# Fewer and wider matmuls per weight block in a hybrid encoder, with the two halves of a sum joined afterwards

## The chip, the core and the metric

The kernel runs on one core of one Trainium2 chip. The metric is the device time of one execution in microseconds, as the median of several runs. The engines have these names in all rows: PE is the matrix engine and PEld its weight load, DVE the vector engine, ACT the scalar engine, POOL the general-purpose one, SP the one that issues most transfers. DMA stands for the 16 transfer engines that all queues share.

## What is computed

Four residual layers over 256 tokens of width 1024, all in float32. Layer i has token mixer i mod 3 (so A, B, C, A), and after it a dense SwiGLU mixer; each has an RMS norm ahead and a residual sum behind.

```python
def short_conv_mixer(h, w_in, conv_w, w_out):              # mixer A
    b_gate, c_gate, u = jnp.split(h @ w_in, 3, axis=-1)
    return (b_gate * depthwise_conv3(c_gate * u, conv_w)) @ w_out

def hyena_mixer(h, w_in, short_w, short_b, ..., w_out):     # mixer C
    v, x1, x2 = jnp.split(depthwise_conv3(h @ w_in, short_w, short_b), 3, axis=-1)
    z = x1 * long_conv(v, 0)
    z = x2 * long_conv(z, 1)
    return z @ w_out

def swiglu(h, w13, w2):
    g, u = jnp.split(h @ w13, 2, axis=-1)
    return (jax.nn.silu(g) * u) @ w2

def reference(x, ...):
    for i in range(DEPTH):                                  # 4
        h = rmsnorm(x, norm_mix_g[i])
        x = x + mixer(i % 3)(h, ...)                        # A, B, C, A
        x = x + swiglu(rmsnorm(x, norm_ffn_g[i]), f_w13[i], f_w2[i])
    return x
```

Mixer B is neighbourhood attention on a 4 x 64 grid. The hidden width of the SwiGLU mixer is 2816. The long convolutions of mixer C use filters that a small network makes from positions.

## The kernel before

Activations lie transposed: 128 features on the partitions, 256 tokens (`T`) along them, eight such tiles for the width of 1024 (`KT`) and 22 for the hidden width (`FT`).

**Split numbers.** Each float32 operand is cut into a rounded part `hi` and a remainder `lo`, both of the type fp32r, and a product is the sum of three: `hi` of the weight with both parts of the input, and `lo` of the weight with the first part. `mm3` (L119) issues these as three matmuls of 256 columns for a block, that is, for one 128x128 piece of a weight. All three add into the same 256 columns of a PSUM bank.

**A weight's way.** `wload` (L96) takes the next of five buffers `st`, and SP issues the transfer of up to 512 KB into it. ACT makes `hi` by a cast (L106). `lo` is made in one of three ways: DVE subtracts (L114 by the helper at L75), POOL does the same, or ACT writes the negative and POOL issues a transfer that reads the weight from memory a second time and adds it (L109, L110). Six buffers each hold `hi` and `lo`, so PE works on one weight while five lie ahead of it. In the SwiGLU mixers of layers 0 and 1, 17% of the weights go to POOL (`POOL_FILTERS`), until the last two output tiles. In mixer C nearly all go the third way (`low_dma`). All others go to DVE.

**Stages.** `ffn` (L265) runs 11 steps `j`, each of four weights (two of the gate, two of the other half) into two banks, `pg` and `pu`, and `gated` follows each: two products with the norm's factor `R` on DVE, Silu on ACT, the product of both on DVE, and the split into `hid`. Then `po` sums 22 blocks for each of the eight output tiles, three weights a tile. `mixer_a` has three weights for each of eight tiles `m` (`ai`), its own `gated`, and then the output projection `OutProj`. `mixer_c` has 24 weights `ci`, each pair followed by `short`, and spectra, gates and inverse transforms between them. In layers 0 and 1 `fill` puts a piece of the filter network (`filters`, tiles `ff`, `fl`, `fh`) behind some steps. In mixer B and in `OutProj` the activations or the sums are laid out otherwise.

**Order.** Eight PSUM banks serve all stages. `Pipeline` puts `gated` and the like behind the weight of a later tick. The instructions stand on each engine in an order that a scheduler makes from the program, and each engine takes its own in that order.

Of the kernel before, what the change touches and what calls it, by code (L numbers as in the profile page):

```python
# [18 lines left out]
P = 128  # L19
D = 1024  # L20
# [26 lines left out]

POOL_FILTERS = 0.17
# [4 lines left out]
def encoder(ctx: ExitStack, tc: tile.TileContext, A: dict, out: bass.AP):  # L53
# [40 lines left out]
    share, count, low_dma = [0], [0], [False]  # L94

    def wload(src, n, tag="", cuts=((0, None, None),)):  # L96
# [5 lines left out]
        for c0, c1, then in cuts:  # L102
# [16 lines left out]
    def mm3(ps, w, ws, xh, xl, first, last, skip=False):  # L119
# [4 lines left out]
        pe.matmul(ps, lo[:, ws], xh, start=False, stop=last, **kw)  # L124

# [139 lines left out]
    def ffn(layer, norm, nxt, fill):  # L265
        with tc.tile_pool(name=f"ffn{layer}", bufs=NP_) as hp:
            hid = []

            def gated(j, pg, pu):
                if j == 0:  # L270
                    norm.expand()
                tg, tu = t2(f"tg{layer}_{j}"), t2(f"tu{layer}_{j}")
                tt(v2(tg), v2(pg), norm.R2(), ALU.mult)
                sg = t2(f"sg{layer}_{j}")
                ac.activation(sg, tg, AF.Silu)
                tt(v2(tu), v2(pu), norm.R2(), ALU.mult)
# [7 lines left out]
            line = Pipeline()
            for j in range(NP_):
                pg, pu = bank(f"pg{layer}_{j}"), bank(f"pu{layer}_{j}")
                parts = []
                for ps, base in ((pg, 0), (pu, FT)):
                    for i in range(2):
                        c = base + 2 * j + i  # L290
                        w = wload(A["f_w13"][layer, c], D, f"w13_{layer}_{c}")
                        parts.append((ps[:, i * T : (i + 1) * T], w, i == 0))
                        if j == 0 and len(parts) == 4:
                            in_group(parts, norm)
                        elif j:
                            in_tile(*parts[-1][:2], norm)
                        line.tick()
                if j == 0:
                    line.add(line.now + NORM_LAG, norm.stats)
                line.add(line.now + (NORM_LAG + 1) * (j == 0), gated, j, pg, pu)  # L300
            while line.todo:
                line.tick()
            for m in range(KT):
# [3 lines left out]
                for k0, k1 in ((0, 8), (8, 15), (15, 22)):  # L307
                    w = wload(A["f_w2"][layer, m][:, k0 * P : k1 * P], (k1 - k0) * P, f"w2_{layer}_{m}_{k0}")
                    for k in range(k0, k1):
                        h = hid[k // 2][:, k % 2]  # L310
                        mm3(ps[:, :T], w, slice((k - k0) * P, (k - k0 + 1) * P), h[:, 0], h[:, 1],
                            k == 0, k == FT - 1)
# [5 lines left out]
    def triple(w, m, norm, name, ready, each=lambda i: None):  # L318


        a, b = bank(f"{name}a{m}"), bank(f"{name}b{m}")
        parts = []
        for i, ps in enumerate((a[:, :T], a[:, T:], b[:, :T])):
            if i == 0 and isinstance(ready, tuple):
                wt = ready
# [611 lines left out]
```

## Time and profile before

| | us |
|---|---|
| median of 3 runs | 1228.61 (1228.05 to 1230.01) |
| the profiled execution | 1226.87 |
| its span in the trace | 1225.1 |
| PE busy in the span | 1206.4 |
| DVE busy | 889.6 |
| ACT busy | 639.5 |
| POOL busy | 186.2 |

The span goes from the first to the last instruction of the trace; 1.8 us of the execution lie outside it. Stages follow each other on PE in this order: mixer A of layer 0 from 6 to 102 us, SwiGLU 0 to 304, mixer B to 425, SwiGLU 1 to 625, mixer C to 750, SwiGLU 2 to 939, mixer A of layer 3 to 1032, SwiGLU 3 to the end. A busy share counts an engine as busy while an instruction runs, so a pipelined engine can be 98% busy and still have room between the starts of its instructions: for PE one reads the distance from start to start.

### The profile page before, as it was taken

To read this page: it belongs to the slowest core of one execution; us is meant where nothing else is said; L and a number is where in the kernel's file an instruction comes from. 1 tells how busy PE (TensorE), PEld (TensorE's weight loads), DVE (VectorE), ACT (ScalarE), POOL (GpSimd) and SP (SyncE) were. 2 spreads that over 40 slices of the span, in tenths; PEclk is the share of its full clock that TensorE was granted. 3 is DMA by queue.
4 is the path that set the end of the run, shared out by engine and by line. 5 is a ranking of instruction groups with operands and counts; after the bars stand their busy time and mean duration, and the time that the engine had idled before them with its cause. 6 is when DMAs were issued, how large, how long until landed. Compare 5 with 4: busy or idle time off the path is not lost.

```text
span 1225.1 us, 24409 instructions
## 1 busy us (share of the span) xinstructions
PE 1206.4 (98%) x10034; PEld 1200.5 (98%) x10034; DVE 889.6 (73%) x1209; ACT 639.5 (52%) x916; POOL 186.2 (15%) x175
## 2 busy tenths in 40 slices
PE   7999999999998999999999999999999999999998
PEld 7999999999998999999999999999999999999998
DVE  7867877988676778788849996766654886766642
ACT  6445554555566655545558675444444444544431
POOL 0001122232454122222322110000000000000000
PEclk9999999999999999999999999999999999999999
DMA  8556656667666456665689995655665655655661
GB/s 316 183 178 206 201 168 207 175 200 223 218 182 188 147 191 187 195 192 175 208 256 288 293 280 192 221 183 178 176 187 173 207 181 161 204 182 186 169 200 44
DMA packets 72104, 242.00 MB, mean 198 GB/s; under 512 B 10231, under 2 KB 11641, under 8 KB 71865
## 3 DMA queue, kind: packets, MB, share of 16 engines
q1 hardware_dynamic: 61408, 211.68, 54.8%
q0 software_dynamic: 8256, 22.84, 8.1%
q10 hardware_dynamic: 2328, 5.93, 1.3%
q8 instruction: 78, 1.28, 0.4%
q14 instruction: 34, 0.27, 0.1%
HBM read 234.10 MB, written 6.29 MB: 196 GB/s over the span
## 4 chain that ended last, share of the span: by engine, by line
PE 91%; DVE 2%; DMA 2%; POOL 2%; ACT 1%; issue 1%; SPq 0%; POOLq 0%; DVEq 0%; ACTq 0%
PE pu L122 7%; PE pg L122 7%; PE pg L124 7%; PE pu L123 7%; PE pg L123 7%; PE pu L124 7%; PE po L124 7%; PE po L123 7%; PE po L122 7%; PE ci L123 2%; PE ci L122 2%; PE ci L124 2%; PE ai1a L123 1%; PE ai1a L122 1%; PE ai1a L124 1%; PE ai0a L123 1%
## 5 line engine op out<-in xcount | busy, mean ns | idle before, releaser
L106 ACT CAST hiw<-stw 128x1024 fp32r<-128x1024 f32 (+1 forms) x276 | 280.5, 1024 | 315.7 <-PE pg L123 82.4
L75 DVE TENSOR_TENSOR low<-stw,hiw 128x1024 fp32r<-128x1024 f32 (+1 forms) x254 | 305.2, 1208 | 156.8 <-ACT hiw L106 155.4
L122 PE MATMUL pu<-xsf,hiw 128*128 128x256 f32 x704 | 199.9, 284 | 0.0
L122 PE MATMUL pg<-xsf,hiw 128*128 128x256 f32 x704 | 199.3, 283 | 0.0
L124 PE MATMUL pg<-xsf,low 128*128 128x256 f32 x704 | 199.2, 283 | 0.0
L123 PE MATMUL pu<-xsf,hiw 128*128 128x256 f32 x704 | 199.2, 283 | 0.0
L123 PE MATMUL pg<-xsf,hiw 128*128 128x256 f32 x704 | 199.2, 283 | 0.0
L124 PE MATMUL pu<-xsf,low 128*128 128x256 f32 x704 | 199.2, 283 | 0.0
L123 PE MATMUL po<-hid,hiw 128*128 128x256 f32 x704 | 197.5, 281 | 0.0
L122 PE MATMUL po<-hid,hiw 128*128 128x256 f32 x704 | 197.5, 281 | 0.0
L124 PE MATMUL po<-hid,low 128*128 128x256 f32 x704 | 197.5, 281 | 0.0
L122 PEld LDWEIGHTS pg<-xsf,hiw 128*128 128x128 f32 x704 | 134.6, 191 | 0.3 <-issue 0.3
L122 PEld LDWEIGHTS pu<-xsf,hiw 128*128 128x128 f32 x704 | 134.5, 191 | 0.3 <-ACT hiw L106 0.3
L124 PEld LDWEIGHTS pg<-xsf,low 128*128 128x128 f32 x704 | 134.6, 191 | 0.0
L123 PEld LDWEIGHTS pg<-xsf,hiw 128*128 128x128 f32 x704 | 134.6, 191 | 0.0
L123 PEld LDWEIGHTS pu<-xsf,hiw 128*128 128x128 f32 x704 | 134.6, 191 | 0.0
L124 PEld LDWEIGHTS pu<-xsf,low 128*128 128x128 f32 x704 | 134.6, 191 | 0.0
L122 PEld LDWEIGHTS po<-hid,hiw 128*128 128x128 f32 x704 | 132.4, 188 | 0.0
L123 PEld LDWEIGHTS po<-hid,hiw 128*128 128x128 f32 x704 | 132.4, 188 | 0.0
L124 PEld LDWEIGHTS po<-hid,low 128*128 128x128 f32 x704 | 132.4, 188 | 0.0
L75 POOL TENSOR_TENSOR low<-stw,hiw 128x1024 fp32r<-128x1024 f32 (+1 forms) x22 | 53.5, 2432 | 215.3 <-ACT hiw L106 207.3
L106 ACT CAST hiai<-stai 128x1024 fp32r<-128x1024 f32 (+1 forms) x49 | 49.0, 1014 | 58.4 <-issue 26.6
(246 smaller groups left out, 2795.4 us busy)
## 6 DMA issues: line engine op xcount, KB each, us to landing
stw<-in_f_w SPq DMA_DIRECT2D x208, 512.0 KB, 3.6
stw<-in_f_w SPq DMA_DIRECT2D x64, 448.0 KB, 3.5
stai<-in_a_w_in SPq DMA_DIRECT2D x45, 512.0 KB, 3.6
stbi<-in_b_w_qkv SPq DMA_DIRECT2D x24, 512.0 KB, 4.3
stci<-in_c_w_in SPq DMA_DIRECT2D x24, 512.0 KB, 8.2
loci<-in_c_w_in POOLq DMA_DIRECT2D x19, 512.0 KB, 16.8
stao<-in_a_w_out SPq DMA_DIRECT2D x16, 512.0 KB, 3.4
hf<-ht POOLq DMA_DIRECT2D x16, 256.0 KB, 2.7
```

The source lines that it names most:

```text
L75: (eng or ve).tensor_tensor(out=out_, in0=a, in1=b, op=op)
L106: ac.copy(out=hi[:, c], in_=st[:, c])
L122: pe.matmul(ps, hi[:, ws], xh, start=first, stop=False, **kw)
L123: pe.matmul(ps, hi[:, ws], xl, start=False, stop=False, **kw)
L124: pe.matmul(ps, lo[:, ws], xh, start=False, stop=last, **kw)
```

## The change

- `mm2` replaces `mm3` in the SwiGLU mixers (both products), in the input products of mixers A and C. A block now has two matmuls: `hi` of the weight with both parts of the input side by side, 512 columns into a whole bank, and `lo` with the first part, 256 columns into the first half. `OutProj`, mixer B and the filter network keep three.
- The second half of the bank has to be added. `join` does it for the input products: ACT copies the half to SBUF, DVE adds the other half to it. For `po` DVE adds both halves to `X` one after the other.
- `ffn` runs 22 steps of two weights, with a bank for the gate and one for the other half. `gated` works on 256 columns where it worked on 512, but for the product with `R`. Mixer A takes three banks for each tile where it took two, mixer C two where it took one.
- No `lo` is made on POOL any more. In the SwiGLU mixers of layers 0 and 1, 34% of the weights (`DMA_FILTERS`) get it from ACT and the adding transfer.

```diff
-POOL_FILTERS = 0.17
+DMA_FILTERS = 0.34
...
-            if low_dma[0]:
+            count[0] += 1
+            if int(count[0] * share[0]) > int((count[0] - 1) * share[0]) and not isinstance(src, list):
                 ac.activation(lo[:, c], st[:, c], AF.Copy, scale=-1.0)
                 gp.dma_start(out=lo[:, c], in_=src[:, c], accum_op=ALU.add)
-                continue
...
+            else:
+                tt(lo[:, c], st[:, c], hi[:, c].bitcast(F32), ALU.subtract)
...
+    def mm2(ps, w, ws, hl, first, last):
+        hi, lo = w
+        pe.matmul(ps, hi[:, ws], hl.rearrange("p s t -> p (s t)"), start=first, stop=False)
+        pe.matmul(ps[:, :T], lo[:, ws], hl[:, 0], start=False, stop=last)
+
+    def join(dst, ps, name):
+        c = t1(name)
+        ac.copy(out=c, in_=ps[:, T:])
+        tt(dst, ps[:, :T], c, ALU.add)
...
-            def gated(j, pg, pu):
+            def gated(j, ps):
...
+                s = t2(f"s{layer}_{j}")
+                for i in range(2):
+                    join(s[:, i * T : (i + 1) * T], ps[i], f"c{layer}_{j}{i}")
+                tt(v2(s), v2(s), norm.R2(), ALU.mult)
+                sg = t1(f"sg{layer}_{j}")
+                ac.activation(sg, s[:, :T], AF.Silu)
+                hh = t1(f"hh{layer}_{j}")
+                tt(hh, sg, s[:, T:], ALU.mult)
...
+                split(pair[-1][:, j % 2], hh)
...
-                        mm3(ps[:, :T], w, slice((k - k0) * P, (k - k0 + 1) * P), h[:, 0], h[:, 1],
-                            k == 0, k == FT - 1)
+                        mm2(ps, w, slice((k - k0) * P, (k - k0 + 1) * P), hid[k], k == 0, k == FT - 1)
+                tt(X[:, m, :], X[:, m, :], ps[:, T:], ALU.add)
                 residual(m, ps[:, :T], nxt)
...
-                tt(v2(bc), v2(a), norm.R2(), ALU.mult)
-                tt(u, b[:, :T], norm.R, ALU.mult)
+                for i, dst in enumerate((bc[:, :T], bc[:, T:], u)):
+                    join(dst, ps[i], f"c{ia}_{m}{i}")
+                tt(v2(bc), v2(bc), norm.R2(), ALU.mult)
+                tt(u, u, norm.R, ALU.mult)
...
-                tt(v2(pr), v2(ps), norm.R2(), ALU.mult)
+                for j in range(2):
+                    join(pr[:, j * T : (j + 1) * T], ps[j], f"c{q}_{i}{j}")
+                tt(v2(pr), v2(pr), norm.R2(), ALU.mult)
```

Three places show how the instructions stand. A row has the line of its own kernel, the operation, what it writes and reads, and the size of what it writes.

On PE, the start of a gate product in SwiGLU 0 (`xsf` is the split input, `hiw13` and `low13` are the parts of a weight). Before:

```order
L122 MATMUL pg0_2_1616<-xsf0_0_1216,hiw13_0_4_1619 128x256
L123 MATMUL pg0_2_1616<-xsf0_0_1216,hiw13_0_4_1619 128x256
L124 MATMUL pg0_2_1616<-xsf0_0_1216,low13_0_4_1620 128x256
L122 MATMUL pg0_2_1616<-xsf0_2_1227,hiw13_0_4_1619 128x256
L123 MATMUL pg0_2_1616<-xsf0_2_1227,hiw13_0_4_1619 128x256
L124 MATMUL pg0_2_1616<-xsf0_2_1227,low13_0_4_1620 128x256
```

Now:

```order
L128 MATMUL pg0_2_1318<-xsf0_0_1104,hiw13_0_2_1321 128x512
L129 MATMUL pg0_2_1318<-xsf0_0_1104,low13_0_2_1322 128x256
L128 MATMUL pg0_2_1318<-xsf0_2_1115,hiw13_0_2_1321 128x512
L129 MATMUL pg0_2_1318<-xsf0_2_1115,low13_0_2_1322 128x256
L128 MATMUL pg0_2_1318<-xsf0_4_1128,hiw13_0_2_1321 128x512
```

Two rows stand where three stood, 2688 times in the program, and the columns of a block are 768 as before.

On DVE, the middle of SwiGLU 2, four weights long (`tg`, `tu` are the two halves times `R`, `hh` the gated product, `hid` the remainder of its split). Before:

```order
L75 TENSOR_TENSOR tg2_6_10499<-pg2_6_10334,Rf2_9759 128x512
L75 TENSOR_TENSOR low13_2_37_10572<-stw13_2_37_10570,hiw13_2_37_10571 128x1024
L75 TENSOR_TENSOR low13_2_16_10604<-stw13_2_16_10602,hiw13_2_16_10603 128x1024
L75 TENSOR_TENSOR tu2_6_10500<-pu2_6_10335,Rf2_9759 128x512
L75 TENSOR_TENSOR hh2_6_10505<-sg2_6_10502,tu2_6_10500 128x512
L75 TENSOR_TENSOR low13_2_17_10645<-stw13_2_17_10643,hiw13_2_17_10644 128x1024
L75 TENSOR_TENSOR hid2_6_10507<-hh2_6_10505,hid2_6_10507 128x2x256
L75 TENSOR_TENSOR low13_2_38_10675<-stw13_2_38_10673,hiw13_2_38_10674 128x1024
```

Now, two weights long (`s` holds the joined halves, `c2` what ACT copied out of a bank):

```order
L74 TENSOR_TENSOR s2_7_9264<-pg2_7_9179,c2_70_9265 128x256
L74 TENSOR_TENSOR s2_7_9264<-pu2_7_9180,c2_71_9268 128x256
L74 TENSOR_TENSOR s2_7_9264<-s2_7_9264,Rf2_8930 128x512
L74 TENSOR_TENSOR low13_2_33_9462<-stw13_2_33_9460,hiw13_2_33_9461 128x1024
L74 TENSOR_TENSOR hh2_7_9274<-sg2_7_9272,s2_7_9264 128x256
L74 TENSOR_TENSOR s2_8_9324<-pg2_8_9240,c2_80_9325 128x256
L74 TENSOR_TENSOR s2_8_9324<-pu2_8_9241,c2_81_9328 128x256
L74 TENSOR_TENSOR hid2_6_9215<-hh2_7_9274,hid2_6_9215 128x256
L74 TENSOR_TENSOR s2_8_9324<-s2_8_9324,Rf2_8930 128x512
L74 TENSOR_TENSOR low13_2_12_9486<-stw13_2_12_9484,hiw13_2_12_9485 128x1024
```

Five small instructions come with two weights where four larger ones came with four, and the sums that free the banks now wait for ACT's copy as well as for PE.

On POOL, a stretch of SwiGLU 0 (`l`, `lr`, `sk`, `eo`, `hf` belong to the filter network). Before:

```order
L75 TENSOR_TENSOR lr00_2385<-l100_2084,lr00_2385 128x256
L75 TENSOR_TENSOR low13_0_14_2345<-stw13_0_14_2343,hiw13_0_14_2344 128x1024
L640 DMA sk00_2392<-in_skip 128x256
L75 TENSOR_TENSOR eo000_2401<-eo000_2401,sk00_2392 128x256
L654 DMA hf00_85<-ht000_2413 128x512
L654 DMA hf00_85<-ht001_2416 128x512
L75 TENSOR_TENSOR low13_0_38_2584<-stw13_0_38_2582,hiw13_0_38_2583 128x1024
```

Now:

```order
L74 TENSOR_TENSOR lr00_2192<-l100_1912,lr00_2192 128x256
L110 DMA low13_0_14_2156<-in_f_w13 128x1024
L110 DMA low13_0_37_2289<-in_f_w13 128x1024
L655 DMA sk00_2199<-in_skip 128x256
L74 TENSOR_TENSOR eo000_2208<-eo000_2208,sk00_2199 128x256
L669 DMA hf00_85<-ht000_2220 128x512
L669 DMA hf00_85<-ht001_2223 128x512
L110 DMA low13_0_17_2374<-in_f_w13 128x1024
```

Adding transfers stand where subtractions stood, twice as many: 22 in SwiGLU 0 and 21 in SwiGLU 1, where POOL subtracted 11 and 10 times.

## Rows read from the trace of the kernel before

**Rows 1.** The page, busy time of each engine, and granted clock over 40 slices

```profile
PE 1206.4 (98%) x10034; PEld 1200.5 (98%) x10034; DVE 889.6 (73%) x1209; ACT 639.5 (52%) x916; POOL 186.2 (15%) x175
...
PEclk9999999999999999999999999999999999999999
```

**Rows 2.** The page, chain that ended last, shares of the span by engine

```profile
PE 91%; DVE 2%; DMA 2%; POOL 2%; ACT 1%; issue 1%; SPq 0%; POOLq 0%; DVEq 0%; ACTq 0%
```

**Rows 3.** Groups of PE instructions: busy us, mean ns, idle before

```profile
L122 PE MATMUL pu<-xsf,hiw 128*128 128x256 f32 x704 | 199.9, 284 | 0.0
...
L123 PE MATMUL po<-hid,hiw 128*128 128x256 f32 x704 | 197.5, 281 | 0.0
```

**Rows 4.** Timeline of PE in two products: start us, length us

```profile
443.12 0.28 PE L124 MATMUL pu<-xsf,low 128*128 128x256 f32 x1
...
443.48 0.28 PE L124 MATMUL pu<-xsf,low 128*128 128x256 f32 x1
...
299.74 0.28 PE L122 MATMUL po<-hid,hiw 128*128 128x256 f32 x1
...
302.09 0.28 PE L124 MATMUL po<-hid,low 128*128 128x256 f32 x1
```

**Rows 5.** Timeline of PE in mixer C, and transposes in the chain

```profile
657.25 1.89 PE L739 MATMUL yi<-a,dfti 128*128 128x256 f32 x8
658.97 0.63 PE L683 MATMUL ut<-ident,cx 128*128 128x128 f32 x4
...
401.93 0.44 PE pqt L446 x4
```

**Rows 6.** Stretches: length, busy PE, PEld, DVE, ACT, POOL, clock, DMA share, GB/s

```profile
102.10:303.90 201.80, 201.42 (x1683) 200.25 (x1682) 165.08 (x213) 106.14 (x144) 50.16 (x40) 1.00 0.63 195
303.90:425.40 121.50, 115.64 (x965) 113.68 (x964) 84.84 (x134) 74.09 (x169) 48.92 (x52) 1.00 0.63 192
...
749.60:939.40 189.80, 189.80 (x1590) 189.80 (x1589) 122.81 (x149) 90.70 (x114) 0.70 (x1) 1.00 0.60 183
939.40:1031.80 92.40, 92.40 (x775) 92.40 (x774) 67.03 (x103) 42.99 (x59) 1.72 (x1) 1.00 0.57 184
```

**Rows 7.** The same for 100 us of mixer C

```profile
645.00:745.00 100.00, 99.38 (x806) 98.22 (x807) 88.99 (x142) 70.85 (x95) 18.16 (x21) 1.00 1.05 291
```

**Rows 8.** Groups of DVE and ACT instructions: busy us, mean ns, idle before

```profile
L75 DVE TENSOR_TENSOR low<-stw,hiw 128x1024 fp32r<-128x1024 f32 (+1 forms) x254 | 305.2, 1208 | 156.8 <-ACT hiw L106 155.4 <-POOL lr L75 1.2
...
L75 DVE TENSOR_TENSOR hh<-sg,tu 128x512 f32<-128x512 f32 x44 | 37.8, 859 | 1.7
...
L75 DVE TENSOR_TENSOR X<-X,po 128x256 f32<-128x256 f32 x32 | 13.4, 418 | 21.0 <-PE po L124 20.9
...
L275 ACT ACTIVATE sg<-tg 128x512 f32<-128x512 f32 x44 | 27.7, 630 | 12.5 <-DVE tg L75 12.4
...
L109 ACT ACTIVATE loci<-stci 128x1024 fp32r<-128x1024 f32 x19 | 20.1, 1056 | 0.0
...
L161 ACT ACTIVATE sqf<-X 128x256 f32<-128x256 f32 x28 | 11.3, 402 | 0.0
...
L185 ACT COPY Rf<-psnf 128x256 f32<-128x256 f32 x4 | 1.5, 368 | 0.0
```

**Rows 9.** Transfers: queues (packets, MB, share), and median us to landing

```profile
q1 hardware_dynamic: 61408, 211.68, 54.8%
q0 software_dynamic: 8256, 22.84, 8.1%
...
loci<-in_c_w_in POOLq DMA_DIRECT2D x19, 512.0 KB, 16.8
```

**Rows 10.** Landing of the one `loci` transfer issued between 637 and 639 us

```profile
DMA to landing us min/median/max: 6.3/6.3/6.3
```

**Rows 11.** Groups of POOL instructions: busy us, mean ns, idle before

```profile
L75 POOL TENSOR_TENSOR low<-stw,hiw 128x1024 fp32r<-128x1024 f32 (+1 forms) x22 | 53.5, 2432 | 215.3 <-ACT hiw L106 207.3 <-PE ff L611 8.0
...
L110 POOL DMA_DIRECT2D loci<-in_c_w_in x19 | 16.5, 870 | 64.2 <-ACT loci L109 61.3 <-ACT cx L343 2.9
```

More of the change, by code (lines that the diff above doesn't have):

```diff
@@ L284, in ffn @@
[L284 to L293, printed above, removed]
+                s = t2(f"s{layer}_{j}")
@@ new lines, in gated @@
+                for i in range(2):
[5 more added lines that the diff above has]
+                tt(hh, sg, s[:, T:], ALU.mult)
+                if j % 2 == 0:
+                    pair.append(hp.tile([P, 2, 2, T], F32R, tag="hid", name=f"hid{layer}_{j}"))
+                split(pair[-1][:, j % 2], hh)
@@ new lines, in gated @@
+                hid.append(pair[-1][:, j % 2])
+                if j % 2:
+                    fill(j // 2)
+            line, pair, parts = Pipeline(), [], []
+            for j in range(FT):
+                ps = [bank(f"pg{layer}_{j}"), bank(f"pu{layer}_{j}")]
+                for i in range(2):
+                    w = wload(A["f_w13"][layer, i * FT + j], D, f"w13_{layer}_{i * FT + j}")
+                    if j < 2:
+                        parts.append((ps[i], w))
+                        if len(parts) == 4:
@@ L301, in ffn @@
+                before = ps
             while line.todo:
@@ L316, in ffn, with triple @@
                 fill(NP_ + m)
[L318 to L325, printed above, removed]
+    def triple(w, m, norm, name, first, each):
+        banks, parts = [], []
+        for i in range(3):
+            if i == 0 and first:
+                wt = first
             else:
-                half = ((0, 512, None), (512, None, None)) if isinstance(ready, tuple) else ((0, None, None),)
+                half = ((0, 512, None), (512, None, None)) if first else ((0, None, None),)
                 wt = wload(w[i * KT + m], D, f"{name}{i}_{m}", half)
-            parts.append((ps, wt, i != 1))
-            if ready:
-                in_tile(*parts[-1][:2], norm)
+            banks.append(bank(f"{name}{i}_{m}"))
+            parts.append((banks[-1], wt))
+            if m or first:
+                in_tile(*parts[-1], norm)
             elif i == 2:
@@ L334, in triple @@
             each(i)
-        return a, b
+        return banks
     def conv3(y, src, wcol, step, m, bcol=None):
@@ L757, in mixer_c @@
                 for q in range(4):
-                    ps = bank(f"ci{q}_{i}")
+                    ps = [bank(f"ci{q}_{i}_{j}") for j in range(2)]
                     for j in range(2):
                         m = 2 * q + j
-                        low_dma[0] = line.now >= LOW_DMA_FROM
+                        share[0] = int(line.now >= LOW_DMA_FROM)
                         w = wload(A["c_w_in"][0][i * KT + m], D, f"ci{i}_{m}")
                         if i == 0 and q < 2:
-                            first.append((ps[:, j * T : (j + 1) * T], w, j == 0))
+                            first.append((ps[j], w))
                             if len(first) == 4:
```

50 lines of the change are left out of this document (18 added, 32 removed).

## The prediction

> **What bounds the kernel now.** I read the busy shares first. PE is busy for 98% of the span at a granted clock of 0.9 or more in every slice (1.00 in all stretches read), the 2.4 GHz level [rows 1, 6]. DVE is at 73% and ACT at 52%. The chain of waits says the same: 91% of it is PE [rows 2]. So time is won only where PE needs less, and lost only where PE comes to wait. PE hardly waits: in SwiGLU 0 it is busy for 201.4 of 201.8 us, in SwiGLU 2 all the time, and mixer B, with 115.6 of 121.5 us, is the worst stage [rows 6].
>
> Busy time can't price a matmul. A matmul runs 281 to 284 ns [rows 3], yet the next starts long before its end. The price is the distance between starts: in the input products 0.36 us for three, 120 ns each; in `po` 2.35 us for twenty, 117.5 ns each [rows 4]. 256 columns at 2.4 GHz make 107 ns, so 11 to 13 ns of each are not stream. A block of three costs 360 ns, or 352 in `po`.
>
> Three stages have something else close behind PE. In SwiGLU 0 DVE is busy for 165.1 of 201.8 us and the transfers have a share of 0.63; in 100 us of mixer C the transfers have a share of 1.05, all 16 engines without a pause, and DVE 89% [rows 6, 7].
>
> **What the change takes from PE.** 2688 blocks go from three matmuls to two: 4 layers of 44 weights by 8 (1408), 4 layers of 8 output tiles by 22 (704), 24 weights by 8 in mixer C (192) and twice as many in the two mixers A (384). The columns stay 768. No row of before has 512 columns of fp32r in one matmul, so I bound it. From below: eight instructions of `yi` take 1.72 us from the first start to the next instruction's, 215 ns each [rows 5]; each has its own weight load and twice the time of a 256-column one, 2 ns over the 213 ns that 512 columns need at 2.4 GHz. From above: twice a matmul of today, 240 ns. What speaks for the lower end is that the gap hardly depends on the stream: transposes of 128 columns start 110 ns apart (0.44 us for four) [rows 5], matmuls of 256 columns 118 to 120 [rows 4]. What both have is a weight load each. If that sets the gap, a long stream hides it, and it is paid only at the 256-column matmul. I take 215 and leave the short matmul at 120 (117.5 in `po`): 335 and 333 ns a block. That saves 25 ns on 1408 + 576 blocks, 49.6 us, and 19.5 ns on 704, 13.7 us: 63.3 us.
>
> For this step the Trainium skill has a rule that speaks against it: "TensorE: Matmul & The Clock Gate", section "Back-to-back issue gap", gives a warm matmul N/2.4 + 2.5 ns, so that only one floor of 2.5 ns goes with each block, 6.7 us in all (an estimate by that page). The trace doesn't agree for 256 columns: it has 118 to 120 ns where the page has 109.
>
> **What of it mixer C gives back.** In its later 100 us transfers are the limit beside PE, and the change leaves their bytes alone: nearly every `lo` is made by the adding transfer, as before. 144 of the 192 blocks lie there, so 144 x 25 ns = 3.6 us are not gained.
>
> **What it adds on DVE and ACT, all beside PE.** A DVE sum of 256 columns from PSUM costs 418 ns, a `lo` 1208 [rows 8]. SwiGLU 0 gets 44 joins (18.4 us), 8 more sums into `X` (3.3), some 1 us for `hh` and `hid` in halves (a half 418, a whole 859), and loses 11 subtractions, since 22 instead of 11 weights go elsewhere (13.3): 165.1 becomes 174.5 us, while the stage shrinks by 352 x 25 and 176 x 19.5 ns to 189.6. DVE is at 92%. SwiGLU 2 gets 122.8 + 24.7 = 147.5 of 177.6 us, 83%. Mixer A of layer 3 gets 24 joins: 77 of 87.6 us, 88%. The 100 us of mixer C get 18 joins: 96.5%. ACT in SwiGLU 0 gets 44 copies at 368 ns, 22 negatives at 1056, and halves (44 x 402 for Silu and cast instead of 22 at 630 and about as much): 106.1 + 16.2 + 23.2 + 8 = 153 us, 81% [rows 6, 8]. POOL drops its subtractions of 2432 ns for issues of 870 [rows 11]. So no engine passes PE on the mean. The transfers of SwiGLU 0 took 0.63 x 201.8 = 127 us; a 512 KB transfer costs 1.7 us by the price of the plain queue (54.8% of the span for 211.7 MB) and 2.3 by that of POOL's queue (8.1% for 22.8 MB) [rows 9], so 22 more make 164 to 177 of 189.6 us, 86 to 93%.
>
> **What nearness costs.** DVE, ACT, POOL and the transfers now have little room at the same time; banks turn over twice as fast (a bank pair served four weights, now two), and ACT's copy stands behind casts that wait for buffers. PE has five weights ahead, 13.4 us, against such waits. No row shows this. From below it costs nothing, as in SwiGLU 0 with DVE at 82%; from above I take mixer B's lost share, 5.9 of 121.5 us, or 4.9% [rows 6]: 9 us for each of SwiGLU 0 and 1, 4 for a mixer A, 5 for C. A gain is excluded, since these stages have next to no wait to lose. I take the middle for SwiGLU 0 and 1 (5 each), which are nearest to the limit; 2 for C, 1.5 for each mixer A, and 0.5 each for SwiGLU 2 and 3: 16 us. At the end of the program one more sum stands on the path, 0.4 us.
>
> **Sum.** 63.3 - 3.6 - 16 - 0.4 = 43.3 us from the profiled 1226.9: 1183.6. The median of the runs lies 1.7 us above that execution, so I forecast 1185.
>
> **Rivals.** (1) *A fixed cost per matmul.* The 11 to 13 ns belong to each matmul, however long. Then 512 columns cost 227 ns (224 in `po`) and a block saves one such cost: 1984 x 13.3 + 704 x 10.8 ns = 34 us. Mixer C gives back 1.9, and with more room the nearness costs 8: 34 - 1.9 - 8 - 0.4 = 23.7, so 1205. For it: `po` and the input products differ by 2 ns with the same weights' shape. Against: `yi` shows 2 ns over its stream. (2) *The gap follows the stream.* 512 columns take twice 256, 236 to 240 ns, and nothing is saved; the joins still cost some 4 us: 1233. For it: only the upper bound of above. Against: 128 columns don't take half of 256. The page's rule named above would end near this rival, at about 1226. (3) *The short matmul gets quicker too*, down to the 110 ns of the transposes: 325 ns a block, 88.8 us, less 5 in mixer C and 20 for nearness: 1165. Nothing in the rows of 256 columns speaks for it. (4) *Late remainders, the slower side.* In SwiGLU 0 and 1, 43 weights now get `lo` by the adding transfer, and PE's second matmul of such a weight waits for it. From the moment a buffer is free PE has five weights, 13.4 us; two ACT passes (1.06 each) leave 11.3 for the transfer. In mixer C such a transfer lands 16.8 us after its issue in the median [rows 9], but there the share is 1.05; one issued into a lighter stretch landed after 6.3 [rows 10]. With shares of 86 to 93% I expect 7 to 11. Each microsecond of mean lateness over 43 weights costs 43 us, so from a landing of 12.3 us on the whole gain is gone; at 12.9 the time is 1185 + 43 x 1.6 = 1254. What also stands on POOL's queue ahead of them, `eo` and `lr`, which wait for DVE and ACT, would work the same way.
>
> **Chances.** Forecast 0.52; (1) 0.25; (2) 0.07; (3) 0.06; (4) 0.10. The range starts at the forecast without any cost of nearness, which is also rival (3): 1165. It ends at rival (1) with the full 16 us, 1214. Outside lie (2) and (4), 0.17. 0.2% (2.5 us) is about what a measurement can tell from no change. Faster by more: forecast, (1), (3) and the mild part of (4), 0.85. Within it: 0.04, from the edges of (2) and (4). Slower: 0.11.
>
> **What would show it.** Steps right: starts of `pg` and `pu` in pairs, about 215 and 120 ns apart, 333 to 336 for two; PE still the chain; SwiGLU 2 about 178 us long and without waits; SwiGLU 0 about 195; mixer C at 122 or more with a transfer share above 1. A distance of 225 to 227 behind a 512-column matmul is rival (1), 236 to 240 rival (2). Waits of PE on a transfer of `low` in SwiGLU 0 and 1 are rival (4); waits on DVE or ACT for a bank would say that nearness costs more than 16 us. The prediction is wrong if the pair of starts is over 350 ns, or if PE's busy share in SwiGLU 0 falls under 90%.

## The result and the profile after

The changed kernel takes 1249.51 us (median of 4 runs, 1245.58 to 1256.49) beside 1228.36 before: a ratio of 1.0175, interval 1.0157 to 1.0192. It is slower by 1.75%, where 1185 was forecast, and lies outside the range of 1165 to 1214. The profiled execution took 1245.58 us, its span is 1243.8, so 18.7 us more than the span before.

The page of the changed kernel: busy time of the engines, granted clock over 40 slices, POOL's transfer queue (packets, MB, share), and the shares of the chain of waits (these answer to [rows 1, 2, 9]).

```profile
PE 1197.6 (96%) x7346; PEld 1067.4 (86%) x7346; DVE 938.6 (75%) x1556; ACT 755.3 (61%) x1295; POOL 167.3 (13%) x196
...
PEclk9999999999899999999998999999999999999999
...
q0 software_dynamic: 14448, 44.60, 17.7%
...
PE 77%; DVE 6%; DMA 6%; issue 5%; POOL 2%; ACT 2%; POOLq 0%; SPq 0%; DVEq 0%; ACTq 0%
```

PE has 2688 matmuls fewer and is busy for only 8.8 us less. Its share of the chain falls from 91% to 77%; DVE and the transfers have what it lost. The queue that carries the adding transfers takes 17.7% where it took 8.1. Two slices show a clock under 0.9, where none did.

The stretches of the changed kernel: SwiGLU 0, mixer B, SwiGLU 1, mixer C, SwiGLU 2, and the input products of SwiGLU 3 (columns: length, busy time of PE, PEld, DVE, ACT, POOL, clock, transfer share, GB/s; as in [rows 6]).

```profile
102.10:306.90 204.80, 198.74 (x1154) 173.18 (x1153) 156.07 (x271) 136.68 (x228) 44.64 (x50) 1.00 0.87 240
306.90:434.30 127.40, 117.22 (x964) 115.69 (x963) 86.59 (x137) 76.81 (x172) 48.74 (x53) 0.97 0.66 194
434.30:633.20 198.90, 195.48 (x1151) 172.52 (x1150) 158.16 (x262) 136.06 (x223) 44.64 (x55) 1.00 0.87 244
633.20:775.20 142.00, 127.94 (x807) 115.31 (x806) 108.83 (x192) 93.49 (x144) 22.23 (x26) 0.95 0.93 247
775.16:962.31 187.15, 186.95 (x1062) 162.58 (x1061) 141.18 (x222) 105.96 (x180) 0.71 (x1) 1.00 0.61 185
1052.45:1177.42 124.97, 124.70 (x710) 108.33 (x709) 100.61 (x166) 75.47 (x139) 0.70 (x1) 1.00 0.59 182
```

The same stretches of the kernel before, for SwiGLU 1, mixer C and the input products of SwiGLU 3:

```profile
425.39:624.96 199.57, 199.57 (x1678) 199.57 (x1677) 160.15 (x197) 103.92 (x137) 55.99 (x46) 1.00 0.62 191
624.96:749.61 124.65, 122.74 (x999) 121.12 (x997) 101.12 (x168) 86.61 (x121) 22.46 (x26) 1.00 1.01 284
1031.75:1158.88 127.13, 127.13 (x1062) 127.13 (x1061) 85.49 (x102) 61.25 (x75) 1.70 (x1) 1.00 0.59 180
```

Read each stretch as busy time of PE plus the rest, its idle time. In mixer C idle time goes from 1.9 to 14.1 us, and PE is busy for 5.2 us more although it has fewer instructions, at a granted clock of 0.95: 17.4 us in all. In mixer B idle time rises by 4.3 us and busy time by 1.6. In SwiGLU 0 PE saves 2.7 us and idles 5.7 more. Only where PE was alone, in SwiGLU 2 and 3, does less work show as less time, and little: SwiGLU 2 goes from 189.8 us [rows 6] to 187.2, and the input products of SwiGLU 3 from 127.1 to 125.0 us for 352 blocks, 6 ns each.

Two blocks of the input products of SwiGLU 3, start and length of each matmul (answers to [rows 4]):

```profile
1099.69 0.40 PE L128 MATMUL pg<-xsf,hiw 128*128 128x512 f32 x1
1099.93 0.28 PE L129 MATMUL pg<-xsf,low 128*128 128x256 f32 x1
...
1100.39 0.40 PE L128 MATMUL pg<-xsf,hiw 128*128 128x512 f32 x1
```

From 1099.69 to 1100.39 are two blocks, 0.35 us each, where three matmuls took 0.36 [rows 4]. The 512 columns hold the next start up for some 0.24 us, not 0.215.

PE's longest waits in the whole changed kernel, but for its start (us in total, times, longest):

```profile
PE yi L760 <- DVE a L74: 6.7, 3, 3.3
PE pqt L461 <- DVE qn L74: 5.5, 1, 5.5
PE pu L129 <- DMA low<-in_f_w: 4.3, 2, 2.8
PE ut L700 <- ACT loci L109: 4.1, 1, 4.1
PE pg L129 <- DMA low<-in_f_w: 3.6, 3, 1.3
PE yi L756 <- DVE a L74: 3.1, 2, 2.4
PE po L129 <- DMA low<-in_f_w: 1.6, 2, 0.9
```

`yi` and `ut` lie in mixer C, `pqt` in mixer B, `low` in SwiGLU 0 and 1 (6.0 and 3.4 us).

Stage lengths of all kernels run, from the first matmul of a stage to the first of the next, in us (the first column from the start of the span; the experiments behind the table say what each kernel is):

| | A, layer 0 | SwiGLU 0 | B | SwiGLU 1 | C | SwiGLU 2 and A | SwiGLU 3 |
|---|---|---|---|---|---|---|---|
| before | 102.1 | 201.8 | 121.5 | 199.6 | 124.6 | 282.1 | 193.4 |
| changed | 102.1 | 204.8 | 127.4 | 198.9 | 142.0 | 277.3 | 191.4 |
| wide matmul in two | 103.5 | 207.8 | 125.2 | 202.2 | 140.1 | 282.7 | 194.4 |
| C undone | 103.3 | 208.4 | 125.4 | 201.2 | 127.0 | 275.3 | 191.6 |
| mask early | 100.0 | 204.9 | 125.4 | 198.9 | 143.3 | 276.3 | 191.5 |
| lengths grouped | 102.5 | 205.9 | 122.3 | 197.6 | 138.6 | 276.3 | 190.1 |
| before, adding transfers | 104.0 | 205.0 | 121.6 | 205.0 | 125.4 | 282.1 | 193.3 |
| changed, no adding transfers | 101.8 | 203.7 | 123.4 | 205.4 | 143.4 | 275.3 | 188.9 |
| C undone but for banks | 102.1 | 208.2 | 127.0 | 201.2 | 128.1 | 275.3 | 189.4 |
| late layers alone | 103.5 | 201.8 | 122.7 | 199.6 | 124.9 | 276.3 | 189.6 |
| late layers and all w13 | 103.9 | 205.4 | 122.1 | 204.8 | 128.7 | 276.8 | 190.0 |

Stages with the same code differ by up to 4 us in layer 0's A and in SwiGLU 0 (204.8 to 208.4 in four of these), by some 2 us in B and SwiGLU 1, and by up to 2.7 in the late stages (188.9 to 191.6 in SwiGLU 3 of five). Smaller differences say nothing by themselves.

### The profile page after: what moved, and what is told of

Same layout as the page of the kernel before. It is cut to its first block, busy times and chain, and to the rows that moved or that the text cites. A ratio compares the mean times of both kernels' runs of the same rounds, so it can differ in the third digit from the quotient of the medians.

```text
span 1243.8 us, 20021 instructions
## 1 busy us (share of the span) xinstructions
PE 1197.6 (96%) x7346; PEld 1067.4 (86%) x7346; DVE 938.6 (75%) x1556; ACT 755.3 (61%) x1295; POOL 167.3 (13%) x196
## 3 DMA queue, kind: packets, MB, share of 16 engines
q0 software_dynamic: 14448, 44.60, 17.7%
## 4 chain that ended last, share of the span: by engine, by line
PE 77%; DVE 6%; DMA 6%; issue 5%; POOL 2%; ACT 2%; POOLq 0%; SPq 0%; DVEq 0%; ACTq 0%
PE pu L128 12%; PE pg L128 12%; PE po L128 12%; PE ai L128 6%; PE pu L129 6%; PE pg L129 6%; PE po L129 6%; DMA low<-in_f_w 3%; PE ai L129 3%; PE ci L128 2%; POOL hrt L74 1%; PE ci L129 1%; DMA bm<-in_rpb 1%; DVE U L74 1%; DVE lobi L74 1%
## 5 line engine op out<-in xcount | busy, mean ns | idle before, releaser
L105 ACT CAST hiw<-stw 128x1024 fp32r<-128x1024 f32 (+1 forms) x276 | 281.1, 1025 | 208.4 <-PE pg L128 70.2
L128 PE MATMUL pu<-xsf,hiw 128*128 128x512 f32 x704 | 254.5, 398 | 0.0
L128 PE MATMUL pg<-xsf,hiw 128*128 128x512 f32 x704 | 254.4, 397 | 0.0
L128 PE MATMUL po<-hid,hiw 128*128 128x512 f32 x704 | 246.5, 393 | 0.0
L128 PEld LDWEIGHTS pu<-xsf,hiw 128*128 128x128 f32 x704 | 132.3, 188 | 31.8 <-DVE s L74 0.3
L128 PEld LDWEIGHTS pg<-xsf,hiw 128*128 128x128 f32 x704 | 132.3, 188 | 30.9
L128 PEld LDWEIGHTS po<-hid,hiw 128*128 128x128 f32 x704 | 132.3, 188 | 29.8 <-DVE hid L74 0.5
L128 PE MATMUL ai<-xsm,hiai 128*128 128x512 f32 x376 | 132.5, 398 | 0.0
L129 PE MATMUL ai<-xsm,loai 128*128 128x256 f32 x376 | 105.2, 280 | 0.0
L128 PE MATMUL ci<-xsm,hici 128*128 128x512 f32 x192 | 72.7, 416 | 0.0
L129 PEld LDWEIGHTS ai<-xsm,loai 128*128 128x128 f32 x376 | 71.0, 189 | 0.0
```

Source lines behind the costliest of these rows:

```text
L105: ac.copy(out=hi[:, c], in_=st[:, c])
L128: pe.matmul(ps, hi[:, ws], hl.rearrange("p s t -> p (s t)"), start=first, stop=False)
L129: pe.matmul(ps[:, :T], lo[:, ws], hl[:, 0], start=False, stop=last)
```

## Experiments

**What a matmul costs.** A kernel of nothing but series of matmuls.

```diff
+    def series(name, n, wt, xt, count=48, alone=False, same=False, second=0):
...
+        for i in range(count):
+            k = 0 if same else i % 8
+            c = (i % 3) * 512
...
+            pe.matmul(ps[:, :n], wt[:, k * P : (k + 1) * P], xt[:, c : c + n], start=first, stop=last and not second)
+            if second:
+                pe.matmul(ps[:, :second], wt[:, k * P : (k + 1) * P], xt[:, c : c + second], start=False, stop=last)
```

> This kernel leaves the whole computation out and only prices matmuls: series of 48 (or 16) TensorE matmuls, each with its own 128x128 weight load, in fp32r with 128 (ra), 256 (rb), 384 (rc) and 512 (rd) columns, 512 and 256 in turn (pair), 512 without accumulation (alone), 512 with one weight throughout (same), bf16 with 256 (hb) and 512 (hd), fp32 with 128 (fa); then 256 and 512 columns beside busy VectorE (dvs, dvl), ScalarE (ats, atl) and transfers (dml, dms, dmm). Theory S, the gap follows the stream: about 0.461 ns a column whatever the width, so 256 columns 118 ns, 384 177, 512 236, and in the pair 354 for two, with nothing else running. Theory F, on which the forecast stood: 215 ns for 512 and 120 for 256. Theory L, neighbours: 215 ns in the quiet series rd and 230 to 241 only beside VectorE, ScalarE or transfers. If accumulation in PSUM is what costs, alone is at 215 and rd at 236; if the four bytes a column are what costs, bf16 with 512 columns is at 215.

Each row is one series: start, length, name, columns, count. The distance of two starts, over the count, is the price of one. The row behind the first is a stretch, with the columns used above.

```profile
15.73 9.68 PE L46 MATMUL warm<-Xr,Wr 128*128 128x512 f32 x42
16.00:25.25 9.25, 9.25 (x43) 7.65 (x42) 9.25 (x9) 9.25 (x10) 0.00 (x0) 1.00 0.00 0
25.25 5.47 PE L46 MATMUL ra<-Xr,Wr 128*128 128x128 f32 x48
30.55 5.97 PE L46 MATMUL rb<-Xr,Wr 128*128 128x256 f32 x48
36.37 8.51 PE L46 MATMUL rc<-Xr,Wr 128*128 128x384 f32 x48
44.71 11.08 PE L46 MATMUL rd<-Xr,Wr 128*128 128x512 f32 x48
55.63 0.39 PE L46 MATMUL pair<-Xr,Wr 128*128 128x512 f32 x1
...
72.58 11.05 PE L46 MATMUL alone<-Xr,Wr 128*128 128x512 f32 x48
83.47 11.04 PE L46 MATMUL same<-Xr,Wr 128*128 128x512 f32 x48
94.36 5.41 PE L46 MATMUL hb<-Xb,Wb 128*128 128x256 bf16 x48
99.61 10.52 PE L46 MATMUL hd<-Xb,Wb 128*128 128x512 bf16 x47
109.97 3.73 PE L46 MATMUL fa<-X,W 128*128 128x128 f32 x32
...
157.77 11.04 PE L46 MATMUL dml<-Xr,Wr 128*128 128x512 f32 x48
```

In fp32r 256 columns cost 5.82/48 = 121 ns, 384 cost 174, 512 cost 10.92/48 = 227.5: 13.8 to 14.6 ns over the stream at 2.4 GHz (106.7, 160, 213.3) whatever the width. In turn, 512 and 256 cost 16.95/48 = 353, and not 227 + 121 = 348. All three theories miss: S has the pair right and each of the rest wrong, and F and L fall with `rd`, beside which nothing runs. The series meant for a busy DVE and ACT don't test L: DVE was through with its work by 31.7 us and idle all through `dvl`, 91 us later. What ran beside busy engines was the first series, `warm`: from 16 us on DVE and ACT are busy without a pause, and 512 columns cost (25.25 - 15.73)/42 = 227 ns. Beside transfers (share 0.81), `dml` has the length of `same`. So neighbours don't change the price. Neither accumulation nor a new weight is the reason (`alone` 227, `same` 227). The type is: bf16 costs 109 and 216, and the 31 entries of `fa` (fp32, 128 columns, two entries a matmul) before its last, of 0.28 us, 3.45/31 = 111. The Trainium skill ("TensorE: Matmul & The Clock Gate", section "Back-to-back issue gap") gives N/2.4 + 2.5 ns for a warm matmul, as the gap of a single isolated one. The bf16 series agree with it; for fp32r the measurement decides, with some 14 in place of the 2.5.

**Where the 5 ns of the pair come from.** The same kernel with other series.

```diff
+    run("pr", [W512, N256])
+    run("bank", [W512, (256, 0, 0, 1)])
+    run("half", [W512, (256, 0, 256, 0)])
+    run("cols", [W512, (256, 256, 0, 0)])
+    run("two", [W512, W512, N256, N256])
+    run("oct", [W512] * 8 + [N256] * 8)
```

> Leaves the whole computation out and prices what the first series of matmuls left over: in turn, 512 and 256 columns took 353 ns for two, though alone they took 227 and 120, 347. Series of 48 fp32r matmuls: pr repeats the pair; bank writes the 256 columns to another bank; half writes them to the bank's other half; cols reads other columns of the moving tile; two goes 512, 512, 256, 256; oct goes eight times 512, then eight times 256; tri goes as the kernel before (three of 256); bpair is the pair in bf16; sml 256 and 128, mid 384 and 256, big 512 and 384 in turn. Theory A, the turn from one length to the other costs 6 ns a pair: bank, half and cols stay at 353, two falls to 350 a pair, oct to 348. Theory P, the short matmul adds onto columns that the wide one has just written: bank and half fall to 347, oct is at 347. Theory R, reading the same moving columns again: cols falls to 347. If bf16 shows it too, the pair is above 216 + 109 = 325.

Series of 24 pairs (or 48 matmuls), start, length, name:

```profile
25.50 8.63 PE L50 MATMUL pra<-Xr,Wr 128*128 128x512 f32 x48
42.46 8.64 PE L50 MATMUL halfa<-Xr,Wr 128*128 128x512 f32 x48
50.94 8.64 PE L50 MATMUL colsa<-Xr,Wr 128*128 128x512 f32 x48
59.42 8.52 PE L50 MATMUL twoa<-Xr,Wr 128*128 128x512 f32 x48
67.78 8.53 PE L50 MATMUL octa<-Xr,Wr 128*128 128x512 f32 x48
76.14 5.92 PE L50 MATMUL tria<-Xr,Wr 128*128 128x256 f32 x48
81.90 7.97 PE L50 MATMUL bpaira<-Xb,Wb 128*128 128x512 bf16 x48
```

From `pra` to `halfa` lie two series, `pr` and `bank`: 16.96/48 = 353 a pair. `half` and `cols` take 353 too (8.48/24), so P and R fall. `two` and `oct` take 8.36/24 = 348: the turn from one length to the other at every matmul costs 5 ns a pair, as A says, and it is gone when the lengths change at every second matmul already (A had 350 there). That holds in this kernel of series; in the whole kernel the turn isn't always paid (see the lengths grouped). bf16 shows none of it (some 322 a pair). What in the engine makes the turn dear stays open.

**The wide matmul alone undone.**

```diff
-        pe.matmul(ps, hi[:, ws], hl.rearrange("p s t -> p (s t)"), start=first, stop=False)
+        pe.matmul(ps[:, :T], hi[:, ws], hl[:, 0], start=first, stop=False, skip_group_check=True)
+        pe.matmul(ps[:, T:], hi[:, ws], hl[:, 1], start=False, stop=False, skip_group_check=True)
```

> The changed kernel with only the wide matmul undone: the 512-column matmul is issued as two of 256 columns into the two halves of the same bank; banks, joins, hidden tiles and adding transfers stay. Theory S: the wide matmul is worth 6.6 ns on each of some 1984 blocks and 1 ns on 704, so some 12 to 14 us are lost: about 1262. Theory W, the wide matmul is itself what made the kernel slower (by holding PE longer at a time): this kernel is faster than the changed one, towards 1235. Theory N: without any effect, 1249 plus or minus 3.

1257.53 us, 1.0235 of before (1.0196 to 1.0274), 8 us over the changed kernel. In the late stages it loses 5.4 and 3.0 us against the changed kernel, 8.4 for 1248 blocks or 6.7 ns each; against the shortest late stages with the same wide matmuls (275.3 and 188.9) it loses 12.9. The wide matmul is a small gain, not the cause of the loss (W falls); S had 12 to 14 us in all, and mixers B and C, 4 us shorter here, hide a part.

**Mixer C as before.**

```diff
-                            in_tile(ps[j], w, norm)
+                            in_tile3(ps[:, j * T : (j + 1) * T], w, norm)
...
-                for j in range(2):
-                    join(pr[:, j * T : (j + 1) * T], ps[j], f"c{q}_{i}{j}")
-                tt(v2(pr), v2(pr), norm.R2(), ALU.mult)
+                tt(v2(pr), v2(ps), norm.R2(), ALU.mult)
```

> The changed kernel with mixer C's input products as before: three 256-column matmuls a block, two weights to a bank, no joins there. Theory J, the joins in mixer C put DVE and ACT on the path (142.0 us against 124.6): the stage goes back to some 125 us and the kernel to 1249.5 - 17 = 1232, with no stretch of half clock in that stage. Theory B, the stage is slow because of what comes before it or because of the transfers: less than 5 us come back, 1245 or more.

1234.73 us, 1.0044 of before (1.0019 to 1.0068): 15 of the 21 us come back, in the stage that was undone (142.0 to 127.0).

**Mixer C as before, but a bank for each weight.** The edit is shown against the kernel of the experiment above.

```diff
-                tt(v2(pr), v2(ps), norm.R2(), ALU.mult)
+                for j in range(2):
+                    tt(pr[:, j * T : (j + 1) * T], ps[j][:, :T], norm.R, ALU.mult)
```

> The changed kernel with mixer C's products in three 256-column matmuls again and without joins, but with a bank for each weight as in the change, so that only the doubled use of banks stays there. Theory J, DVE's and ACT's work in the 24 joins (10 and 9 us) is what made mixer C 15 us longer: the stage takes 127 us as with everything undone there, the kernel 1234.7. Theory K, banks that turn over twice as fast: the stage stays at some 140 us, the kernel at 1247 or more.

1233.92 us, 1.0053 of before (1.0032 to 1.0075). Mixer C of three kernels: with joins and 256-column matmuls alone (the wide matmul in two); without joins, with its own banks; without both.

```profile
638.75:778.83 140.08, 127.46 (x998) 124.83 (x997) 108.56 (x192) 93.06 (x144) 22.22 (x26) 0.96 0.94 249
...
638.40:766.49 128.09, 124.42 (x998) 123.31 (x997) 102.15 (x180) 86.70 (x120) 22.31 (x26) 0.97 0.99 274
...
638.23:765.21 126.98, 124.16 (x998) 122.56 (x997) 102.10 (x169) 86.64 (x121) 22.27 (x26) 0.99 1.00 278
```

The first two have the same number of matmuls and the same banks. They differ by the 24 joins and by the half of the bank that one product goes to, and in what the stages ahead do: 12 us. K falls, J holds.

The wait that comes and goes with the joins is PE's for `a`, a tile that DVE makes on the way from one transform to the next: 9.8 us in the changed kernel, 8.4 with the wide matmul in two, none in the two kernels without joins and none before. DVE has only 108.6 of 140 us to do, but this mean hides where. Behind the first 30 us of the stage it was all but full already: 71.9 of 75 us in the kernel before. With the joins DVE has more to do there and also waits for ACT, 6.6 us in 79, most of it for `cx`. DVE in the kernel before and in the changed one, and its longest wait there:

```profile
655.00:730.00 75.00, 75.00 (x606) 74.04 (x605) 71.93 (x119) 54.33 (x75) 13.86 (x16) 1.00 1.05 289
...
670.00:749.00 79.00, 69.08 (x418) 60.92 (x417) 72.25 (x125) 53.25 (x83) 12.86 (x15) 0.96 0.99 262
...
DVE cx L358 <- ACT cx L357: 4.7, 4, 2.0
```

The wait of 4.1 us for `ut`, transposes that stand ahead of more `ci` in PE's order, isn't the joins'. It is there without them too, when each weight has its own bank; with everything undone, and before, it is 0.8 us. Why `ut` is late where each weight has its own bank stays open. The wait costs twice: behind it, from 653 to 656 us of the changed kernel, the granted clock is 0.50, the 1.2 GHz level, and PE counts as busy. The wait without joins, and the stretch of the changed kernel:

```profile
PE ut L708 <- ACT cx L366: 3.7, 1, 3.7
...
653.00:656.00 3.00, 3.00 (x11) 2.52 (x11) 1.85 (x5) 3.00 (x5) 0.90 (x2) 0.50 1.05 264
```

**The mask of mixer B loaded early.**

```diff
-            mask = cp.tile([P, 4, P], F32, name="mask")
-            ac.dma_start(out=mask, in_=A["mask"])
...
+    mask = const.tile([P, 4, P], F32, name="mask")
...
+    ac.dma_start(out=mask, in_=A["mask"])
```

> The changed kernel with the attention mask loaded at the program's start into a tile of its own, not on ScalarE's queue at the start of mixer B. Theory M, the late mask (issued 2.9 us into the stage and landed 10.8 us into it, against 0.2 and 5.2 before) delays POOL's queue and by that qn and the transposes pqt: mixer B goes from 127.4 us back to some 121.5 and the kernel to 1243.5. Rival: the stage is longer because of VectorE's or ScalarE's own backlog from SwiGLU 0, then nothing is gained, 1249 plus or minus 2.

1242.46 us, 1.0117 of before (1.0085 to 1.0149). The total is as M says, the place isn't: mixer B only falls to 125.4 us. POOL's first `bm` sum then waits for its other input. POOL's waits in the first 30 us of mixer B, changed kernel and this one:

```profile
POOL bm L74 <- DMA mask<-in_mask: 8.6, 1, 8.6
...
POOL bm L74 <- DMA bm<-in_rpb: 7.1, 1, 7.1
```

So M is half right: both transfers are late. Over all kernels, the start of that first sum, counted from the stage's start, and PE's wait for `qn` go together:

| | before | adding transfers alone | grouped | all w13 | late layers | no adding transfers | C undone | wide in two | mask early | C's banks | changed |
|---|---|---|---|---|---|---|---|---|---|---|---|
| first `bm` after, us | 5.4 | 5.1 | 5.9 | 6.5 | 6.5 | 7.2 | 8.6 | 9.2 | 9.4 | 10.7 | 10.9 |
| PE waits for `qn`, us | 0 | 0 | 0.5 | 1.1 | 1.2 | 1.9 | 3.2 | 3.9 | 4.0 | 5.3 | 5.5 |
| transfer share of the first 10 us | 0.68 | 0.66 | 0.73 | 0.68 | 0.67 | 0.73 | 0.85 | 0.91 | 0.89 | 0.87 | 0.87 |

Each microsecond of delay beyond 5.4 is one microsecond of PE. The late kernels are those whose transfers are busiest at the turn of the stage. Whether these are weights that SwiGLU 0 fetched late was not tried.

**The adding transfers alone, and the change without them.**

```diff
-POOL_FILTERS = 0.17
+DMA_FILTERS = 0.34
...
-            if low_dma[0]:
+            count[0] += 1
+            if low_dma[0] or (int(count[0] * share[0]) > int((count[0] - 1) * share[0]) and not isinstance(src, list)):
...
-            tt(lo[:, c], st[:, c], hi[:, c].bitcast(F32), ALU.subtract, gp if pool else ve)
+            tt(lo[:, c], st[:, c], hi[:, c].bitcast(F32), ALU.subtract)
```

> The kernel before with one part of the change alone: in SwiGLU 0 and 1 each third remainder is made by ScalarE and an adding transfer, where POOL subtracted each sixth. Theory T: these transfers are what lengthens SwiGLU 0 by 3.0 us and mixer B by 4 to 6 us in the changed kernel (waits of PE on low, the first transfers of B landing late): 1229 + 6 to 9 = 1235 to 1238. Rival: they fit beside PE as long as joins don't fill VectorE and ScalarE, then 1229 plus or minus 2, or a little under where POOL's queue was late.

1236.42 us, 1.0068 of before (1.0043 to 1.0093). The total is theory T's, in SwiGLU 0 and 1 (205.0 us each, waits of 3.3 us for `low` in either); mixer B is untouched at 121.6, so they alone don't delay it. The 3.2 us in SwiGLU 0 are no more than its spread, but PE's waits are direct.

> The changed kernel with the remainders of SwiGLU 0 and 1 as before the change: POOL subtracts each sixth, VectorE the others, no adding transfer there. Theory T: the adding transfers cost what they cost alone in the kernel before, 7.7 us (205.0 us instead of 201.8 and 199.6 in the two SwiGLUs), and they also fill the first 10 us of mixer B (transfer share 0.87 against 0.67): the kernel falls by 8 to 12 us to 1238 to 1241, and no PE wait on low is left. Theory V: with 44 joins beside them VectorE (85% in SwiGLU 0 then, from 76%) and POOL become what PE waits for, and nothing is gained: 1248 or more.

1241.49 us, 1.0100 of before (1.0083 to 1.0118), 8 us under the changed kernel, and no wait for `low`: the total is about theory T's. The two profiled executions differ by only 1.8 us (1243.81, the longest of this kernel, and 1245.58, the shortest of the other), and in mixed directions: mixer B 4.0 shorter, SwiGLU 1 6.5 longer. There V's mechanism holds: DVE is at 184.9 of 205.4 us, and PE waits for it at the first output products (SwiGLU 1):

```profile
PE po L129 <- DVE hid L74: 5.2, 1, 5.2
```

So it seems that the joins need the room which the adding transfers make on DVE, and that these cost about as much as they bring.

**The lengths grouped.** For each weight first its wide matmuls, then its short ones.

```diff
-            mm2(ps, w, slice(k * P, (k + 1) * P), xs, n == 0, n == KT - 1)
+            wide(ps, w, slice(k * P, (k + 1) * P), xs, n == 0)
+        for n, (k, xs) in enumerate(norm.xs.items()):
+            short(ps, w, slice(k * P, (k + 1) * P), xs, n == KT - 1)
```

> The changed kernel with the matmuls of a weight in another order: first its wide matmuls (eight, or seven in the output products), then its short ones, so that the two lengths hardly alternate, and the remainder is wanted later. Theory A (the turn costs 6 ns a block): 2688 blocks less 6 ns, less C's 192, are 15 us, and the waits on the adding transfers (some 9.5 us in two SwiGLUs) go too: 1227 to 1235. Theory P or R would give the same 15 us; if the order doesn't matter, the matmul gaps stay at 353 a block and only the waits on the transfers go: 1240 to 1249.

1236.29 us, 1.0059 of before (1.0042 to 1.0075), 13 us under the changed kernel. Most of it is mixer B (5 us) and C (3 us), where waits became shorter. A has the size of the total, and not its places: the input products of SwiGLU 3 take 123.8 us (125.0 changed, 127.1 before), 3 ns a block less where it had 6.

That even these 3 ns come from the order isn't shown. With the changed kernel's order the same products take 125.2 and 125.3 us in two other kernels (C undone, mask early) and 123.0 in two more (C's banks, no adding transfers). Here are that stretch with C's banks, and the first and last start of three blocks in SwiGLU 1 of the changed kernel itself, (501.29 - 500.25)/3 = 0.347 us each:

```profile
1041.80:1164.81 123.01, 122.74 (x710) 107.22 (x709) 100.56 (x166) 75.44 (x139) 0.70 (x1) 1.00 0.59 185
...
500.25 0.39 PE L128 MATMUL pu<-xsf,hiw 128*128 128x512 f32 x1
...
501.29 0.39 PE L128 MATMUL pu<-xsf,hiw 128*128 128x512 f32 x1
```

So in the whole kernel the turn from 512 to 256 columns is paid in some stages and not in others, with the same instructions. What decides it stays open.

**Only where there is room.** The kernel before, with grouped pairs in SwiGLU 2 and 3 and layer 3's mixer A.

```diff
-            mixer_a(layer // 3, norm, nf, False if layer else first)
+            (mixer_a2 if layer in (3,) else mixer_a)(layer // 3, norm, nf, False if layer else first)
...
-            ffn(layer, nf, norm, fill)
+            (ffn2 if layer in (2, 3) else ffn)(layer, nf, norm, fill)
```

> The kernel before with two matmuls a block only where nothing else is near its limit: both products of SwiGLU 2 and 3 and the input products of layer 3's mixer A, wide matmuls of a weight first, then its short ones. SwiGLU 0, 1, the mixers B, C and layer 0's A stay. By the stage lengths of the runs so far: SwiGLU 2 with mixer A 276.3 us instead of 282.1, SwiGLU 3 190.1 instead of 193.4, so 9 us less: 1228.7 - 9 = 1220, 0.993 of before. If the gain in these stages came from what lay before them, 1226 or more.

1222.56 us, 0.9943 of before (0.9929 to 0.9957): the fastest kernel here, 6.7 us under the kernel before, where 9 were expected. The changed stages have the lengths expected (276.3, 189.6); in the profiled execution layer 0's A and mixer B, whose code is the same, were 1.4 and 1.2 us longer. That the grouping has a part in the gain isn't shown: ungrouped, the same products have taken 123.0 us as well. Input products of SwiGLU 3:

```profile
1028.77:1152.62 123.85, 123.61 (x710) 108.56 (x709) 101.93 (x167) 75.88 (x140) 0.70 (x1) 1.00 0.57 185
```

**And the input products of SwiGLU 0 and 1.** The same, with `ffn2` for all layers, `po` in three matmuls and the remainders as before.

> As the kernel with the late layers alone, and beside them the products with w13 in SwiGLU 0 and 1 in the same order; the output products of every SwiGLU stay in three matmuls, and the remainders of layers 0 and 1 are made as before, by VectorE and POOL. If the joins hide: 352 blocks less 10 ns in each of SwiGLU 0 and 1, 7 us, less 1.8 us in the output products of layers 2 and 3: 1220 - 5 = 1215. If VectorE's 18 us of joins in SwiGLU 0 and 1 come onto the path, 1222 or more.

1234.78 us, 1.0043 of before (1.0030 to 1.0056). SwiGLU 0 and 1 take 205.4 and 204.8 us, 3.6 and 5.2 more than before, with DVE at 184.6 of 205.3: the joins come onto the path. PE's longest waits there are for results of `gated` or of the filter network from DVE and ACT: 3.4 us for `s` in SwiGLU 0, 3.7 us for `hid` in SwiGLU 1.

## Why the prediction was wrong

**What bounds the kernel** was right: PE, and where nothing else is near, SwiGLU 2 and 3, the gain on PE is the gain of the stage.

**The price of 512 columns** is the first step that failed. I took 215 ns from `yi` [rows 5], since a weight load seemed to set the gap. But `yi` is fp32, in two entries a matmul; the matmuls at hand are fp32r, which cost some 14 ns over their stream from 256 columns on (227 ns for 512), and in turn with 256 columns often another 5. So a block takes 353 ns, or 347 where the turn isn't paid, and not 335. It saves 6 to 12 ns where I had 25. At 353 throughout, that is some 13 us on 1984 blocks, not 49.6. For `po` (before 0.353 us a block by [rows 4]) I had 13.7; its stretch in SwiGLU 3 is 66.4 us against 66.2, so nothing. Rival (1) had the right mechanism and 227 ns, and lacked the turn. Rival (2) had 236 to 240, for a reason that `rd` refutes. A pair of starts over 350 ns, which I had named as the sign that the prediction is wrong, is what came in SwiGLU 3.

**Mixer C** is the second step that failed, the term for nearness. It was to give back 3.6 us for its transfers and 2 for nearness. It lost 17.4 and its own gain of 1.3. The transfers didn't hold it (share 0.93 after, 1.01 before). The joins did: some 12 us by the kernels with and without them, lower clock included. I had priced them by a mean of DVE over 100 us, 89% before and 96.5% after [rows 7]. In 75 of these 100 us DVE was at 96% before the joins came, and the sums that came on top made PE wait for `a`.

**Mixer B** had no term, as no line of it changes. It lost 5.9 us, most of it by two late transfers at its start; what made them late stays open.

**SwiGLU 0 and 1**, at 5 us each for nearness, were near: 5.7 and 3.4 us more idle time. But the waits are those of rival (4), for `low`, 9.4 us in all where it put 43 us on each microsecond: the landing was 8.1 us in the median, within the 7 to 11 expected. PE's busy share in SwiGLU 0 stayed at 97%. That joins and transfers each cost about as much alone was not seen. DVE, forecast at 92% of SwiGLU 0, came to 76% (156.1 of 204.8 us), because it lost more than the 11 subtractions: where POOL no longer subtracts, DVE's own instructions on SBUF are shorter (`hh` 1010 ns before, 684 with the adding transfers alone).

**SwiGLU 2, 3 and layer 3's A** cost nothing for nearness, where 2.5 us were set. DVE's added work in SwiGLU 2 is 22.7 us by the prediction's own terms (18.4, 3.3 and 1), not 24.7; it came to 18.4 (141.2 less 122.8). And the forecast without any nearness is 1169, so the range began at rival (3) alone, 1165. Neither slip bears on the miss.

**The sum as it should have been**: 13 us from the blocks, less 18.7 in C, 5.9 in B, and 5.3 and 1.6 in SwiGLU 0 and 1 (their share of the 13, 2.3 each, and what their length says) is 18.5 slower; the spans say 18.7. (The stages are those of one profiled execution, and the 13 us an estimate at 353 ns a block.) Layer 0's A brings nothing of its 1.3, and the late layers 1 us more than their blocks; that is within what stages vary.

## What to carry to other kernels

Price a matmul by a row of its own type, and if the change brings a width or an alternation that no row shows, let the range cover a cost per matmul that stays. An edit that moves work from the engine that bounds the kernel to others pays only in stages without a chain through those others: make it there alone, as the fastest kernel here does. A free share is no room when the mean hides a stretch in which the engine is full, or when each of its results is waited for. And a wait of a few microseconds can be paid a second time: 4.1 us for `ut` in mixer C were followed by a stretch at half the clock.

## What the runs showed of the hardware

- In a stream of matmuls, fp32r costs 13.8 to 14.6 ns over N/2.4 GHz at 256, 384 and 512 columns; bf16 2.5 to 2.7; an fp32 entry 215 ns for 256 columns [rows 5] and 111 for 128. 128 columns of fp32r cost 110 (5.30/48), twice their stream. 512 columns cost the same 227 ns alone, beside busy DVE and ACT, and beside transfers.
- fp32r matmuls of 512 and 256 columns in turn cost 353 ns a pair in the kernel of series, in groups of two or eight 348; another bank, another half or other moving columns change nothing. In the whole kernel the pair cost about 353 in some stages and 347 in others.
- Behind waits of PE the granted clock was 0.50: after 4.1 us in mixer C from 653 to 656 us, and after 5.5 us for `qn` in mixer B from 338 to 340 us. There matmuls of 256 columns start 0.21 us apart (256 columns at 1.2 GHz), and at 340.83 and 340.95 us 0.12 apart again.
- With POOL subtracting in SwiGLU 0 (no adding transfers), DVE's `hh`, which reads SBUF alone, takes 661 ns in the mean; in the changed kernel, where POOL doesn't subtract, 421. A join's sum, which reads PSUM, takes 417 and 419.
